# Where a projection stage issues its stores, and into which tiles it writes the lower halves of k

## The chip, the cores and the metric

The kernel runs on one core of one Trainium2 chip. The metric is the device time of one execution in microseconds. Engines are named as in the profile: PE (TensorE matmul), DVE (VectorE), ACT (ScalarE), POOL (GpSimd) and SP (SyncE, which here only issues DMAs); each works through its own instructions in order.

## The reference

One step of a one-layer streaming encoder over 1024 prompt tokens and 64 sample tokens, all in float32. What matters here is its first part, the combined input projection, and what is done at once with q and k:

```python
xn = _rmsnorm(x, p['norm_mix_w'])
proj = xn @ p['w_in']
z, xbc, dt_raw, q, k, v, gate_ssm, gate_att = jnp.split(proj, np.cumsum(IN_SIZES)[:-1].tolist(), axis=-1)
...
y_ssm = y_ssm * jax.nn.silu(z)
...
q = _partial_rope(_rmsnorm(q.reshape(b, t, 2 * ATT_HEADS, ATT_HEAD_DIM), p['q_norm_w']), q_pos)
k = _partial_rope(_rmsnorm(k.reshape(b, t, 2 * ATT_HEADS, ATT_HEAD_DIM), p['k_norm_w']), q_pos)
```

k after norm and rotation is also an output. q and k, and the cached keys, are used later by the attention, which this kernel multiplies in split precision: a float32 array is held as an upper half (cast to TensorE's rounded type) and a lower half (the rest).

## The kernel before

**The stage of pairs.** q, k and z are projected in 16 pairs of 256 output columns (`in_pair`, L636), q first, then k, then z. A pair is a two-by-two blocked product made of seven block products instead of eight, each in two column ranges s, so it has 14 steps; a step is 12 matmuls (`pile`, L642: four blocks of the inner dimension by three terms upper-upper, upper-lower, lower-upper) into one PSUM bank. Step by step the results are combined: p0 is copied by ACT into u1 (L685), p1 is added by DVE into u2 (L687), p3 into u1 (L689), and p2, p4, p5, p6 give the four finished blocks of a pair (ACT L695, DVE L697) in tiles `pre`. p2 and p3 go on accumulating into the banks of p0 and p1, so PE can start them only after L685 and L687 have read what stands there.

**The weights** of the next pair are loaded by SP (L552), combined by POOL (`ws` and `w_f`, L563 to L569), and split by ACT (cast to `wh` or `w_hi`, L419) and DVE (the rest, to `wh` or `w_lo`, L420).

**Finished rows.** `done` (L660) applies Silu to a finished block of z (L666), or adds the squares of q's and k's rows up (L673 to L677), and stores the block to a DRAM scratch: `z_sc`, `q_r` or `k_r` (L678, 64 stores of 272 KB, issued by SP).

**Norm, rotation and split of q, k and the cached keys** ride beside the pairs that follow. `finishing` (L802) and `cached_keys` (L876) make one generator `job` (L760) per piece: 24 pieces of 128 rows (`part`, twelve of q and twelve of k), 8 of two row blocks that are rotated (`turned`, four each), and 8 of cached keys. A job fetches its rows into a tile x on POOL's queue (L830; L846 and, for the rotation's cosines, L847; L880), waits four turns, scales x on DVE (L834, or L854 and the rotation L858 to L861, with a helper tile rt), stores it, for k alone, as the output `kT` (L769, on SP), waits a turn, casts the upper half on ACT (L773) into a tile xh (or rt), stores it (L774, SP, 40 stores), waits two turns (four for k), subtracts in place on DVE to leave the lower half in x (L777), and stores that (L778, SP). For k, L777 therefore waits until the store of x to the output has read x. A turn is one step of a pair; `take_turn` (L782) advances every running job at each step.

**Tiles.** `row(tag, name)` (L476) hands out 1088 columns of a ring of buffers: "fx" has four (x, and n1), "fc" three (xh, sq, rt, rp and others), "fp" three (`pre`). A tile's first writer waits for the last reader of the tile that had the buffer before. The order on each engine is as the steps record it, except that `after(...)` (L161) pins a block's instructions behind the named ones recorded last.

**Semaphores of DMAs.** The DMAs of SP and ACT take turns in eight semaphores, so an issue also waits for the one some eight issues before it to have landed.

Of the kernel before, what the change touches and what calls it, by code (L numbers as in the profile page):

```python
# [9 lines left out]
F32 = mybir.dt.float32  # L10
R32 = mybir.dt.float32r
# [6 lines left out]
P = 128  # L18
# [72 lines left out]
def hybrid_layer(ctx: ExitStack, tc: tile.TileContext, xT, xt, prm, cst, rope, wvd, win, wbs, wba, wout, wup, wdn,  # L91
# [2 lines left out]
    V, S, G, PE = nc.vector, nc.scalar, nc.gpsimd, nc.tensor  # L94
    act = S.activation
    load = nc.sync.dma_start

    dram = ctx.enter_context(tc.tile_pool(name="dram", bufs=1, space=DRAM))
    cp = ctx.enter_context(tc.tile_pool(name="cp", bufs=1))
# [376 lines left out]
    def row(tag, name, dt=F32):  # L476
        if tag in ("fa", "fs", "fu"):
            w = {"fa": KT * P, "fs": 4 * P, "fu": HT}[tag]
            return rows_l.tile([P, w], dt, name=name, tag=tag, bufs=IN_ROWS[tag])
        w = {"ss": T}.get(tag, HT)  # L480
        return rows_r.tile([P, w], dt, name=name, tag=tag, bufs=IN_ROWS[tag])
# [154 lines left out]
    def in_pair(n):  # L636

        kind, j = INPUT[n]
        u1, u2 = row("fx" if n == 1 else "fu", "u1"), row("fu", "u2")
        banks, out = {}, {}  # L640

        def pile(key, p, s, start):  # L642
            if start:
                banks[key, s] = acc(W2[s])
            ps, w, b = banks[key, s], left[n][p], parts[PARTS[p], s]
            for k in range(4):
                c = slice(P * k, P * (k + 1))
                for i, (x, y) in enumerate(((0, 0), (0, 1), (1, 0))):
                    seen["mm"] = PE.matmul(ps, w[x][:, c], b[y][:, k], start=start and k == i == 0, stop=k == 3 and i == 2,
                                           skip_group_check=not start)  # L650
            return ps

        def to(r, c, s):

            if (r, c) not in out:
                out[r, c] = row("fp", "pre")
            a, w = O2[s], W2[s]
            return out[r, c][:, a : a + w]

        def done(r, c):  # L660
            cs = slice(HT * c, HT * (c + 1))
            t = out[r, c][:, :HT]
            f = 2 * j + r
            if kind == "z":
                with after("root"):
                    seen["silu"] = act(t, t, AF.Silu)  # L666
            else:
                if kind not in squares:
                    squares[kind] = row("ss", "ss")
                ss = squares[kind][:, cs]  # L670
                if (kind, c) not in begun_squares:
                    begun_squares.add((kind, c))
                    act(ss, t, AF.Square)  # L673
                else:
                    sq = row("fc", "sq")[:, :HT]
                    act(sq, t, AF.Square)
                    V.tensor_tensor(out=ss, in0=ss, in1=sq, op=ALU.add)  # L677
            load(out={"z": z_sc, "q": q_r, "k": k_r}[kind][P * f : P * (f + 1), cs], in_=t)  # L678

        at = yield  # L680
        for _ in range(14):
            p, s = at
            us = cols(s)
            if p == 0:
                seen["copy"] = S.copy(u1[:, us], pile("a", p, s, True))  # L685
            elif p == 1:
                seen["read"] = V.tensor_tensor(out=u2[:, us], in0=pile("b", p, s, True), in1=u1[:, us], op=ALU.add)  # L687
            elif p == 3:
                seen["read"] = V.tensor_tensor(out=u1[:, us], in0=pile("b", p, s, False), in1=u1[:, us], op=ALU.add)  # L689
            else:  # L690
                r, c, key, start, u = {2: (0, 0, "a", False, None), 4: (1, 1, "c", True, u1), 5: (1, 0, "d", True, u1),
                                       6: (0, 1, "c", False, u2)}[p]
                ps = pile(key, p, s, start)
                if u is None:
                    seen["copy"] = S.copy(to(r, c, s), ps)  # L695
                else:
                    seen["read"] = V.tensor_tensor(out=to(r, c, s), in0=ps, in1=u[:, us], op=ALU.add)  # L697
                if s == 1:
                    ripe.append(lambda r=r, c=c: done(r, c))
            at = yield  # L700
# [56 lines left out]
                    return  # L757
            yield 2

    def job(fetch, scale, hi_of, hi_rows, lo_rows, keep=None):  # L760

        x = fetch()
        yield 4
        hi = lambda: None
        if scale is not None:
            with after("read"):
                x = scale(x)
            if keep is not None:
                load(out=keep, in_=x)  # L769
            yield 1  # L770
        with after("copy"):
            hi = hi_of()
            S.copy(hi, x)  # L773
        load(out=hi_rows, in_=hi.bitcast(F32))  # L774
        yield 2 if keep is None else 4
        with after("read"):
            V.tensor_tensor(out=x.bitcast(R32), in0=x, in1=hi, op=ALU.subtract)  # L777
        load(out=lo_rows, in_=x)  # L778

    running, clock = [], [0, 0, 0]  # L780

# [20 lines left out]
    def finishing(kind):  # L802

        d, to, keep, wcol = {"q": (q_r, q_st, None, lambda j: wq8[:, j : j + 1]),
                             "k": (k_r, k_st, kT, lambda j: col(O_KN + j))}[kind]
        rs = squares[kind]
        for (c, w), gap in zip(WIDE, (2, 2, 1)):
            ps = stat(w)
            with tc.issue_after(seen["mm"].ins):
                PE.matmul(ps, blk, rs[:, c : c + w], start=True, stop=True)  # L810
            with after("copy"):
                S.copy(rs[:, c : c + w], ps)
            yield gap
        while kind == "k" and clock[2] not in (6, 7, 8):
            yield 1
        with after("copy", *(["silu"] if "silu" in seen else [])):
            table = S.preload_act_table_set(LN_EXP)
        with tc.issue_after(table.ins):
            for c, w in WIDE:
                t = [row("fx", "n1") for _ in range(2)]  # L820
                rstd_of(None, rs[:, c : c + w], rs[:, c : c + w], w, "qn", 1.0 / 64, t=t)
        yield 3

        def rows_at(y, r0, j, n, c, w):
            return y[r0 + P * j : r0 + P * (j + n), c : c + w].rearrange("(j p) t -> p j t", p=P)

        def part(j, c):
            def fetch():
                x = row("fx", "x")
                G.dma_start(out=x, in_=d[P * j : P * (j + 1), c : c + HT])  # L830
                return x

            def scale(x):
                V.scalar_tensor_tensor(x, x, wcol(j), rs[:, c : c + HT], ALU.mult, ALU.mult)  # L834
                return x.unsqueeze(1)

            at = j, 1, c, HT
            return job(fetch, scale, lambda: row("fc", "xh", R32)[:, :HT].unsqueeze(1), rows_at(to, 0, *at), rows_at(to, D, *at),
                       None if keep is None else rows_at(keep, 0, *at))

        def turned(c):
            t = None

            def fetch():
                x, cosine = couple(row("fx", "x")), couple(row("fc", "rp"))
                G.dma_start(out=x, in_=d[0 : 2 * P, c : c + QW].rearrange("(j p) t -> p j t", p=P))  # L846
                G.dma_start(out=cosine, in_=rope[:, :, c : c + QW])  # L847
                return x, cosine

            def scale(both):  # L850
                nonlocal t
                x, cosine = both
                for j in range(2):
                    V.scalar_tensor_tensor(x[:, j], x[:, j], wcol(j), rs[:, c : c + QW], ALU.mult, ALU.mult)  # L854
                co, si = (cosine[:, i].unsqueeze(1).to_broadcast([P, 2, QW]) for i in range(2))
                t = row("fc", "rt")
                y = couple(t)
                V.tensor_tensor(out=y, in0=x, in1=si, op=ALU.mult)  # L858
                V.tensor_tensor(out=x, in0=x, in1=co, op=ALU.mult)
                V.tensor_tensor(out=x[:, 0], in0=x[:, 0], in1=y[:, 1], op=ALU.subtract)  # L860
                V.tensor_tensor(out=x[:, 1], in0=x[:, 1], in1=y[:, 0], op=ALU.add)  # L861
                return x

            at = 0, 2, c, QW
            return job(fetch, scale, lambda: couple(t.bitcast(R32)), rows_at(to, 0, *at), rows_at(to, D, *at),
                       None if keep is None else rows_at(keep, 0, *at))

        for j in range(2, KT):
            yield part(j, 0)
            yield part(j, HT)  # L870
            yield 1
        for c in range(0, T, QW):
            yield turned(c)
            yield 2
# [1095 lines left out]
```

## Time and profile before

| | us |
|---|---|
| median of 3 runs | 2435.89 |
| lowest and highest of them | 2434.46, 2437.45 |
| the profiled execution's own time | 2433.65 |
| its span | 2431.9 |
| PE busy in the span | 2390.7 |
| DVE, ACT, POOL busy | 1716.9, 1213.1, 692.3 |
| mean granted clock of TensorE | 0.996 of full speed |

The stage of pairs lies between about 115 and 481 us of the span. The profile counts an instruction of an engine as busy; idle time just before it is shown in square brackets in the timeline, with what ended it. DMA-issuing instructions stand on the issuing engine's queue (`SPq`, `POOLq`), with the time that the issue took there; "us to landing" is from the issue to the arrival of the data. Line numbers are those of the kernel before.

### The profile page before, as it was taken

How to read it: one execution, taken by the hardware profiler on the slowest of the kernel's cores; microseconds unless marked ns; L12 is line 12 of the kernel's file. 1: busy time of each engine (PE TensorE's matmuls, PEld its weight loads, DVE VectorE, ACT ScalarE, POOL GpSimd, SP SyncE). 2: the span in 40 equal slices, each digit the busy share in tenths (PEclk: the TensorE clock that was granted, in tenths of full speed). 3: DMA queues.
4: the chain of work that ended last, by engine and by line, in shares of the span. 5: the costliest groups of instructions: out<-in, count | busy, mean ns of one | idle time of the engine just before them, and what ended most of it. 6: DMA issues, size and time to landing. Idle time of an engine off the chain costs nothing. (4 is left out here: it accounts for less than half of the span.)

```text
span 2431.9 us, 49445 instructions
## 1 busy us (share of the span) xinstructions
PE 2390.7 (98%) x18744; PEld 2317.6 (95%) x18744; DVE 1716.9 (71%) x3090; ACT 1213.1 (50%) x2683; POOL 692.3 (28%) x757
## 2 busy tenths in 40 slices
PE   8999999999999999999999999999999999999998
PEld 8999999999999999998899998999999999999998
DVE  4678887668687786867678665756866756777765
ACT  7344454356565665657655553434444333353442
POOL 0032433201011010115343332013254554443344
PEclk9999999999999999999999999999999999999999
DMA  7863768665444444336797954664124424357975
GB/s 244 278 236 129 268 204 302 197 194 155 155 150 152 127 149 142 108 127 227 261 329 248 334 177 162 213 210 159 56 85 147 156 97 157 126 185 211 254 182 105
DMA packets 296240, 449.79 MB, mean 185 GB/s; under 512 B 36729, under 2 KB 192514, under 8 KB 296002
## 3 DMA queue, kind: packets, MB, share of 16 engines
q1 hardware_dynamic: 284962, 420.31, 52.3%
q0 software_dynamic: 11040, 26.34, 5.3%
q8 instruction: 147, 2.41, 0.4%
q14 instruction: 91, 0.75, 0.1%
HBM read 294.03 MB, written 152.50 MB: 184 GB/s over the span
## 5 line engine op out<-in xcount | busy, mean ns | idle before, releaser
L170 PE MATMUL mm<-b,w_hi 128*128 128x272 f32 x1576 | 465.8, 296 | 0.0
L172 PE MATMUL mm<-b,w_lo 128*128 128x272 f32 x1576 | 459.3, 292 | 0.0
L171 PE MATMUL mm<-b,w_hi 128*128 128x272 f32 x1576 | 458.0, 291 | 0.0
L170 PEld LDWEIGHTS mm<-b,w_hi 128*128 128x128 f32 x1576 | 296.9, 188 | 6.2 <-issue 5.1
L171 PEld LDWEIGHTS mm<-b,w_hi 128*128 128x128 f32 x1576 | 297.1, 189 | 2.9 <-issue 2.1
L172 PEld LDWEIGHTS mm<-b,w_lo 128*128 128x128 f32 x1576 | 296.5, 188 | 0.7 <-issue 0.2
L996 DVE SCALAR_TENSOR_TENSOR cc<-pre,par,cc 128x272 f32<-128x272 f32 (+1 forms) x288 | 140.0, 490 | 16.0 <-ACT cc L994 13.0
L1612 PE MATMUL mx<-n,wh 128*128 128x272 f32 x1080 | 144.9, 290 | 1.9 <-DVE u L1639 1.2
L1612 PE MATMUL mx<-m,w_hi 128*128 128x272 f32 x752 | 144.6, 289 | 0.2 <-DVE m L420 0.2
L984 POOL COPY pre<-pre 128x3 f32<-128x3 f32 x72 | 22.9, 318 | 418.5 <-DVE cc L998 198.4
L1612 PEld LDWEIGHTS mx<-n,wh 128*128 128x128 f32 x1080 | 139.7, 190 | 2.3 <-DVE u L1639 1.4
L170 PE MATMUL mx<-b,w_hi 128*128 128x272 f32 x472 | 138.8, 294 | 1.1 <-ACT w_hi L155 0.5
L172 PE MATMUL mx<-b,w_lo 128*128 128x272 f32 x472 | 137.7, 293 | 1.0 <-DVE w_lo L156 1.0
L1120 ACT ACTIVATE p_t<-sc,mx 128x512 f32<-128x512 f32 (+6 forms) x144 | 106.2, 740 | 64.4 <-DVE mx L1111 30.7
L156 DVE TENSOR_TENSOR w_lo<-w_f,w_hi 128x1024 fp32r<-128x1024 f32 (+1 forms) x82 | 102.2, 1247 | 50.6 <-ACT w_hi L155 49.6
L420 DVE TENSOR_TENSOR wh<-w_f,wh 128x512 fp32r<-128x512 f32 (+1 forms) x144 | 136.7, 950 | 0.7 <-ACT wh L419 0.7
L171 PE MATMUL mx<-b,w_hi 128*128 128x272 f32 x472 | 135.8, 288 | 0.0
L155 ACT CAST w_hi<-w_f 128x1024 fp32r<-128x1024 f32 (+1 forms) x82 | 85.9, 1048 | 70.0 <-PE mm L171 49.3
L1612 PEld LDWEIGHTS mx<-m,w_hi 128*128 128x128 f32 x752 | 118.1, 188 | 0.4 <-DVE m L420 0.4
L563 POOL TENSOR_TENSOR ws<-w_f 128x512 f32<-128x512 f32 (+1 forms) x47 | 63.1, 1342 | 176.4 <-DMA w_f<-in_wdn_dram 61.7
L1621 ACT ACTIVATE cc<-pre,par 128x544 f32<-128x544 f32 (+1 forms) x44 | 37.2, 846 | 147.9 <-DVE pre L1656 147.2
L1612 PE MATMUL mx<-m,w_lo 128*128 128x272 f32 x376 | 108.3, 289 | 0.0
(460 smaller groups left out, 7074.3 us busy)
## 6 DMA issues: line engine op xcount, KB each, us to landing
w_f<-in_win_dram SPq DMA_DIRECT2D x48, 512.0 KB, 4.3
w_f<-in_wup_dram SPq DMA_DIRECT2D x80, 256.0 KB, 2.6
bc<-a_sc SPq DMA_DIRECT2D x32, 512.0 KB, 5.6
w_f<-in_win_dram SPq DMA_DIRECT2D x60, 256.0 KB, 3.8
b<-y_sc SPq DMA_DIRECT2D x24, 544.0 KB, 8.3
h_sc<-hb SPq DMA_DIRECT2D x44, 272.0 KB, 2.1
ht<-h_sc SPq DMA_DIRECT2D x22, 544.0 KB, 4.5
t_sc<-ht SPq DMA_DIRECT2D x22, 544.0 KB, 2.9
```

The costliest lines, as they stand in the source:

```text
L155: S.copy(hi, w)
L156: V.tensor_tensor(out=lo, in0=w, in1=hi, op=ALU.subtract)
L170: PE.matmul(ps, a_hi, b_hi, start=i == 0, stop=False)
L171: PE.matmul(ps, a_hi, b_lo, start=False, stop=False)
L172: PE.matmul(ps, a_lo, b_hi, start=False, stop=i == n - 1)
L420: V.tensor_tensor(out=lo, in0=src, in1=hi, op=ALU.subtract)
L563: G.tensor_tensor(out=s1, in0=q21, in1=q22, op=ALU.add)
L984: G.tensor_copy(pre[:, 0:3], tail)
L996: V.scalar_tensor_tensor(cc[:, :m], pre[:, i : i + m], cw(i), cc[:, :m], ALU.mult, ALU.add)
L1120: act(p_t[:n, :nk], sc[c][:n, :nk], AF.Exp, bias=mx[:n, c : c + 1], accum_out=dst)
L1612: PE.matmul(ps, w[x][:, c], b[y][:, k], start=start and k == i == 0, stop=k == 3 and i == 2, skip_group_check=not start)
L1621: act(cc[:, :n], pre[h][:, :n], AF.Identity, bias=col(O_FB + f), scale=cw(0))
```

## The change

Four things, all in the stage of pairs:

- the 64 stores of finished rows (L678) are issued by ACT instead of SP;
- the 40 stores of upper halves (L774) are issued by ACT, pinned behind the cast as the cast is pinned;
- k's lower halves (L777) go into a tile of their own, `xl`: from the ring "fc" for the twelve pieces of 128 rows, from "fx" for the four rotated ones; the subtraction then stands two turns behind the cast for k as for the others, and no longer writes the tile that the store to `kT` reads;
- the stores left on SP stand a turn later: that of `kT` a turn behind the scale, that of the lower half a turn behind the subtraction.

```diff
+    send = nc.scalar.dma_start
...
-            load(out={"z": z_sc, "q": q_r, "k": k_r}[kind][P * f : P * (f + 1), cs], in_=t)
+            send(out={"z": z_sc, "q": q_r, "k": k_r}[kind][P * f : P * (f + 1), cs], in_=t)
...
-    def job(fetch, scale, hi_of, hi_rows, lo_rows, keep=None):
+    def job(fetch, scale, hi_of, hi_rows, lo_rows, keep=None, lo_of=None):
...
                 x = scale(x)
+            yield 1
             if keep is not None:
                 load(out=keep, in_=x)
-            yield 1
         with after("copy"):
             hi = hi_of()
             S.copy(hi, x)
-        load(out=hi_rows, in_=hi.bitcast(F32))
-        yield 2 if keep is None else 4
+            send(out=hi_rows, in_=hi.bitcast(F32))
+        yield 2
+        lo = x if lo_of is None else lo_of()
         with after("read"):
-            V.tensor_tensor(out=x.bitcast(R32), in0=x, in1=hi, op=ALU.subtract)
-        load(out=lo_rows, in_=x)
+            V.tensor_tensor(out=lo.bitcast(R32), in0=x, in1=hi, op=ALU.subtract)
+        yield 1
+        load(out=lo_rows, in_=lo)
...
-                       None if keep is None else rows_at(keep, 0, *at))
+                       *(() if keep is None else (rows_at(keep, 0, *at), lambda: row("fc", "xl")[:, :HT].unsqueeze(1))))
...
-                       None if keep is None else rows_at(keep, 0, *at))
+                       *(() if keep is None else (rows_at(keep, 0, *at), lambda: couple(row("fx", "xl")))))
```

The changed kernel's lines stand one to three further on (L777 is L779 there, L774 is L775, L858 is L861). PE's order is the same but for two places where a handful of its instructions stand a few places off. SP's program goes from 1286 rows to 1180, ACT's from 1978 to 2091.

DVE before, at the end of a pair beside which k is split: the last products' sums into `pre` (L697), then the splits of the next weights, then the sums L687 that PE waits for.

```order
L777 TENSOR_TENSOR x<-x,xh 128x544
L697 TENSOR_TENSOR pre<-mx,u_4378 128x272
L420 TENSOR_TENSOR wh<-w_f,wh 128x512
L834 SCALAR_TENSOR_TENSOR x<-x,par,ss 128x544
L777 TENSOR_TENSOR x<-x,xh 128x544
L420 TENSOR_TENSOR w_lo<-ws_4523,w_hi 128x512
L420 TENSOR_TENSOR w_lo<-w_f,w_hi 128x512
L687 TENSOR_TENSOR u_4648<-mm,u_4647 128x272
```

The same place after.

```order
L698 TENSOR_TENSOR pre<-mx,u_4378 128x272
L421 TENSOR_TENSOR wh<-w_f,wh 128x512
L779 TENSOR_TENSOR xl<-x,xh 128x544
L837 SCALAR_TENSOR_TENSOR x<-x,par,ss 128x544
L421 TENSOR_TENSOR w_lo<-ws_4526,w_hi 128x512
L421 TENSOR_TENSOR w_lo<-w_f,w_hi 128x512
L688 TENSOR_TENSOR u_4653<-mm,u_4652 128x272
```

One of the two subtractions has moved behind L687, and the other stands ahead of the scale and writes `xl`. Next, ACT before, at the end of the pair in which the last pieces of 128 rows meet the first rotated ones of k.

```order
L419 CAST wh<-w_f 128x512 x2
L773 CAST xh<-x 128x544
L666 ACTIVATE pre<-pre 128x544
L773 CAST xh<-x 128x544
L666 ACTIVATE pre<-pre 128x544 x2
L685 COPY u_5191<-mm 128x272
L419 CAST w_hi<-ws_5067 128x512
```

The same place after.

```order
L420 CAST wh<-w_f 128x512 x2
L774 CAST xh<-x 128x544
L775 DMA k_st<-xh 128x544
L667 ACTIVATE pre<-pre 128x544
L679 DMA z_sc<-pre 128x544
L774 CAST xh<-x 128x544
L667 ACTIVATE pre<-pre 128x544
L775 DMA k_st<-xh 128x544
L679 DMA z_sc<-pre 128x544
L667 ACTIVATE pre<-pre 128x544
L679 DMA z_sc<-pre 128x544
L686 COPY u_5204<-mm 128x272
```

Five DMA issues now stand between the casts and the copy of p0. The second cast takes its buffer of "fc" from the first cast's tile (the two buffers between went to an `xl` and to the cosines rp), so it waits until the first store has landed. Last, DVE before, two pairs further on than the first place, where the second rotated piece of k is finished.

```order
L854 SCALAR_TENSOR_TENSOR x<-x,par,ss 128x272 x2
L858 TENSOR_TENSOR rt<-x,rp 128x544
L859 TENSOR_TENSOR x<-x,rp 128x544
L777 TENSOR_TENSOR x<-x,rt 128x544
L860 TENSOR_TENSOR x<-x,rt 128x272
L861 TENSOR_TENSOR x<-x,rt 128x272
L689 TENSOR_TENSOR u_5191<-mx,u_5191 128x272 x2
L697 TENSOR_TENSOR pre<-mx,u_5191 128x272
```

And after.

```order
L857 SCALAR_TENSOR_TENSOR x<-x,par,ss 128x272 x2
L779 TENSOR_TENSOR xl<-x,rt 128x544
L861 TENSOR_TENSOR rt<-x,rp 128x544
L862 TENSOR_TENSOR x<-x,rp 128x544
L690 TENSOR_TENSOR u_5204<-mx,u_5204 128x272
L863 TENSOR_TENSOR x<-x,rt 128x272
L864 TENSOR_TENSOR x<-x,rt 128x272
L690 TENSOR_TENSOR u_5204<-mx,u_5204 128x272
L698 TENSOR_TENSOR pre<-mx,u_5204 128x272
```

The subtraction stands ahead of the next piece's rotation, and the first sum of p3 stands ahead of the rotation's last two instructions.

## The prediction

> **What bounds the kernel.** The page first: the span, and the busy time of the engines.
>
> ```profile
> span 2431.9 us, 49445 instructions
> PE 2390.7 (98%) x18744; PEld 2317.6 (95%) x18744; DVE 1716.9 (71%) x3090; ACT 1213.1 (50%) x2683; POOL 692.3 (28%) x757
> ```
>
> PE works 98% of the time, and the change takes no matmul away. It can only win time in which PE stands still in the stage of pairs, or add to it. So the second view is what PE waits for there, 110 to 490 us (columns: total us, times, longest).
>
> ```profile
> PE mx L649 <- DVE u L687: 3.9, 2, 2.4
> PE mx L649 <- DVE pre L697: 2.7, 2, 2.4
> PE mm L649 <- DVE u L687: 1.4, 1, 1.4
> ```
>
> All the other waits of that list are 1.0 us or less each. The third view, PE's timeline, gives these three rows four places of size (start, duration; in brackets the idle time just before).
>
> ```profile
> 309.37 0.89 PE L649 MATMUL mx<-t,wh 128*128 128x272 f32 x5 [2.35 <-DVE u L687]
> 377.66 0.52 PE L649 MATMUL mm<-t,wh 128*128 128x272 f32 x2 [1.35 <-DVE u L687]
> 421.82 0.89 PE L649 MATMUL mx<-t,wh 128*128 128x272 f32 x5 [1.56 <-DVE u L687]
> 433.54 0.60 PE L649 MATMUL mx<-b,w_hi 128*128 128x272 f32 x2 [2.40 <-DVE pre L697]
> ```
>
> The last one costs more than its idle time. The windows behind it (length, PE busy with its matmuls, granted clock, DMA share, GB/s), and one behind the gap of 309:
>
> ```profile
> 433.50:437.00 3.50, 3.46 (x16) 0.55 1.01 314
> 437.00:441.00 4.00, 4.00 (x33) 0.97 0.77 262
> 309.40:313.00 3.60, 3.60 (x29) 1.00 0.82 250
> ```
>
> Behind 2.40 us of idle the granted clock was 0.55 for 3.5 us, and 16 matmuls took 3.46/16 = 0.216 us each where they take 4.00/33 = 0.121 next: 16 x 0.095 = 1.5 us. Behind 2.35 us it stayed at 1.00. So the four places are worth 2.35 + 1.35 + 1.56 + 2.40 + 1.5 = 9.2 us, 0.38% of the time, and that is the ceiling of this change. A measurement of this kernel can tell about 0.2%, 4.9 us, from no change.
>
> The Trainium skill ("TensorE: Matmul & The Clock Gate", "What's actually happening") has the clock halved after an idle window of about 3.4 us. Here 2.40 us were enough, with less idle than the rule names; by the rule no gap of this size would cost clock, the ceiling would be 7.7 us, and no term of 1.5 us would stand below.
>
> **The change part by part.**
>
> *k's lower half in its own tile.* DVE's waits from 340 to 455 us, and DVE's timeline ahead of the gap at 377:
>
> ```profile
> DVE x L777 <- DMA out_dram<-x: 18.2, 8, 4.5
> ...
> 369.86 0.77 DVE L834 SCALAR_TENSOR_TENSOR x<-x,par,ss 128x544 f32<-128x544 f32 x1
> 374.43 1.62 DVE L777 TENSOR_TENSOR x<-x,xh 128x544 fp32r<-128x544 f32 x1 [3.80 <-DMA out_dram<-x]
> 377.18 0.43 DVE L687 TENSOR_TENSOR u<-mm,u 128x272 f32<-128x272 f32 x1
> ```
>
> L777 overwrites x, so it waits until the store of x has landed, and L687 stands behind it. Eight such waits come to 18.2 us of DVE, but DVE is 71% busy, and PE only stood still behind three of them. In the new order one subtraction stands behind L687 and the other is no longer bound to that store. Its new bound is its buffer of "fc", that is the store of an upper half some jobs earlier. If that comes late it delays L687 as before, but 3.80 us of wait stand against a gap of 1.35, so 2.4 us of it may remain. I take the whole gap: **-1.35** (bounds -1.35 and 0).
>
> *The gap at 433.* DVE's timeline ahead of it:
>
> ```profile
> 424.16 0.91 DVE L854 SCALAR_TENSOR_TENSOR x<-x,par,ss 128x272 f32<-128x272 f32 x2 [0.75 <-DMA x<-k_r]
> 426.24 0.72 DVE L858 TENSOR_TENSOR rt<-x,rp 128x544 f32<-128x544 f32 x1 [1.17 <-DMA rp<-in_rope_dram]
> 428.44 1.14 DVE L777 TENSOR_TENSOR x<-x,rt 128x544 fp32r<-128x544 f32 x1 [0.71 <-DMA out_dram<-x]
> 430.94 1.50 DVE L861 TENSOR_TENSOR x<-x,rt 128x272 f32<-128x272 f32 x1
> 433.07 0.42 DVE L697 TENSOR_TENSOR pre<-mx,u 128x272 f32<-128x272 f32 x1
> ```
>
> From L854 to L697 the chain holds 0.75 + 1.17 + 0.71 = 2.63 us of waits, each for a transfer, against a gap of 2.40. The 0.71 goes with the tile. x and the cosines are fetched by POOL once buffers of "fx" and "fc" are free; x's buffer no longer waits for the lower half's store, so 0.75 should go; the cosines' 1.17 may stay. But in the new order L689 also passes L860 and L861, one of them 1.50 us long. 0.71 + 0.75 + 1.50 = 2.96 is over 2.40, so the gap goes, and its half clock: -2.40 - 1.5 = **-3.9** (bounds -3.9 and 0).
>
> *ACT as issuer.* No DMA is issued from ACT in this trace, so the price must come from SP's rows of the same stores (ns: least, median, most), beside the time that ACT now waits, 110 to 490 us:
>
> ```profile
> L774 SPq DMA_DIRECT2D q_st<-xh x12: 319/323/1745, 248.8 to 299.6; - x12
> L774 SPq DMA_DIRECT2D k_st<-xh x12: 319/587/1034, 351.5 to 413.8; - x12
> L678 SPq DMA_DIRECT2D z_sc<-pre x32: 319/333/842, 311.5 to 482.2; - x32
> ...
> ACT wh L419 <- POOL ws L567: 48.2, 14, 6.5
> ACT w_hi L419 <- POOL w_f L565: 15.2, 6, 3.5
> ```
>
> 104 issues at 0.32 to 0.59 us are 33 to 61 us; over 16 pairs 6.5 issues and 2.1 to 3.8 us a pair. ACT waits 48.2/14 = 3.4 us for POOL's `ws` nearly once a pair, and six times 2.5 us for `w_f`. These waits cover the issues, so I take **0** for them; without that cover they would be 2.1 us a pair. Below zero they do not go by themselves: SP is freed of its waits, but what it loads sooner, the weights, are waited for by POOL and ACT, not by PE.
>
> *The gap at 422.* Here the change adds a wait. ACT's two casts, DVE's rows up to L687, and from 280 to 455 us the landing of an upper half's store (median from the issue):
>
> ```profile
> 409.81 0.64 ACT L773 CAST xh<-x 128x544 fp32r<-128x544 f32 x1
> 410.92 0.63 ACT L773 CAST xh<-x 128x544 fp32r<-128x544 f32 x1
> ...
> 417.32 1.61 DVE L777 TENSOR_TENSOR x<-x,xh 128x544 fp32r<-128x544 f32 x1 [3.18 <-DMA out_dram<-x]
> 418.86 0.71 DVE L858 TENSOR_TENSOR rt<-x,rp 128x544 f32<-128x544 f32 x1
> 421.34 0.43 DVE L687 TENSOR_TENSOR u<-mx,u 128x272 f32<-128x272 f32 x1
> ...
> k_st<-xh SPq DMA_DIRECT2D x12, 272.0 KB, 4.1
> ```
>
> Now the second cast waits for the landing of the first store, and L858 takes its rt buffer from the second cast's tile and waits for the landing of that one's store. The first cast ends at 410.45; + 4.1 = 414.55; the second cast 0.64, and Silu's slot behind it about 0.6: issue at 415.8, landing 419.9. From L858's start to L687's end it is 421.34 + 0.43 - 418.86 = 2.91 us, so L687 ends at 422.8 instead of 421.77: the wait for `kT` (3.18) is gone, and two landings in a row take its place. **+1.0**, a gap of 2.6. Behind ACT's waiting cast stand z's Silu and stores, and behind these the copy L685 and the `w_hi` casts of the next pair; DVE's L420 and L687 wait for those. Bounds: -1.56, if weights and pieces run ahead by the DVE time saved, and +3.0, with both landings a us longer.
>
> *The gap at 309.* The same, beside q, whose tiles haven't changed:
>
> ```profile
> 299.63 0.74 SPq L774 DMA_DIRECT2D q_st<-xh  x1
> 306.69 1.67 DVE L858 TENSOR_TENSOR rt<-x,rp 128x544 f32<-128x544 f32 x1 [1.49 <-DMA q_st<-xh]
> ...
> q_st<-xh SPq DMA_DIRECT2D x2, 272.0 KB, 5.6
> ```
>
> L858 waited for that store to land, 7.0 us after its issue. ACT issues it behind a Square and a store of k_r, about 301.3. With the 5.6 us that the two stores of 296 to 310 us took in the median it lands at 306.9: **+0.3**. Bounds: -2.35 if it lands in 5 us or less, +1.7 with the 7.0 us again.
>
> The Trainium skill ("DMA: Bandwidth & Descriptors", "Issuing engines are not separate DMA queues") says that issuing from several engines only saves the sequencer's time, since all run on the same DMA engines. By that a store issued 1.7 us later lands 1.7 us later, and this term would be the +1.7 and the sum below -1.05. No run here shows an issue from ACT yet.
>
> *Half clock.* Of two gaps of 2.35 and 2.40 one was followed by it. With two expected at about 2.6 I count it once: **+1.5**.
>
> **Sum**: -1.35 - 3.9 + 0 + 1.0 + 0.3 + 1.5 = -2.45 us. Against the profiled execution's own 2433.65 (2.2 below the median, its span 1.75 below itself) that is 2431.2; on the scale of the median, 2435.89 - 2.45 = **2433.4**.
>
> **The rivals.**
>
> *All gaps behind the removed wait go.* If the chain at 410 runs ahead of time, the gap at 422 goes too: -1.35 - 1.56 - 3.9 = -6.8, 2429.1; with the one at 309, 2426.7. For it: 18.2 us of DVE's waits go, and SP's queue loses these (110 to 490 us), so that weights and lower halves behind them are issued sooner.
>
> ```profile
> SPq L774 <- ACT xh L773: 37.3, 14, 6.0
> SPq L678 <- ACT pre L666: 30.7, 17, 7.6
> SPq L678 <- DVE pre L697: 28.3, 21, 3.3
> ```
>
>  Against it: the two landings in a row at 410 are there whatever else runs ahead.
>
> *Nothing moves.* The lower halves wait for their buffer in a ring of three which xh, rt, rp and now xl share, and DVE stands as long as before, for `k_st<-xh` instead of `out_dram<-x`: 0, 2435.9. For it, the store of an upper half lands in 4.1 us, not much sooner than that of x in the same list:
>
> ```profile
> out_dram<-x SPq DMA_DIRECT2D x16, 272.0 KB, 5.1
> ```
>
> Against it, one subtraction has left its place ahead of L687.
>
> *ACT becomes what is late.* An issue waits in ACT's order for its semaphore's earlier DMA; a wait of one landing (4.1) a pair on top of 2.1 us of issues, less the cover of 3.4, leaves ACT 2.8 us late, and with it the copies L685 and the `w_hi` casts, on which L420, L687 and PE stand. It decides as soon as ACT's delay in a pair exceeds 3.4 us. Beside k DVE has gained 18.2/8 = 2.3 a pair to set against it, beside q nothing: two pairs there at 2.8 with a half clock each are +8.6, with the sum above +6.2: 2442.
>
> **How the numbers follow.** The forecast, small gains against two later gaps: 0.30. All gaps go: 0.27. Nothing moves: 0.15. ACT late: 0.28. Faster by over 0.2% (under 2431.0) is the second alone, 0.27; within 0.2% the first and third, 0.45; slower (above 2440.8) 0.28. The range goes from the full gain, 2427.0, to 2443.0, a little over the third rival's price; a twentieth is left below and a seventh above, for more pairs than two. The forecast's own bounds are 2429 to 2437.
>
> **What would show it.** Right: no `out_dram<-x` among DVE's releasers for L777; no gap near 377 and 433; the ones near 309 and 422 still there, behind L687, with `q_st<-xh` and `k_st<-xh` as releasers of L858 and of the cast L773. Wrong on the fast side: those two gone. Wrong on the slow side: PE waiting for ACT's u L685 or for L420 once a pair, ACT idle before its issues, and windows with a granted clock of about half. The matmuls of the rest of the program should take what they took.

## The result, and the profile after

| | before | after |
|---|---|---|
| median of 22 runs, us | 2434.40 | 2429.14 |
| lowest and highest, us | 2427.17, 2438.01 | 2423.21, 2433.48 |
| ratio of the two, 95% interval | | 0.9982 (0.9975 to 0.9989) |
| profiled execution's own time, span, us | 2433.65, 2431.9 | 2427.86, 2426.1 |
| first matmul of the stage of pairs to the end of its last, us | 115.74 to 480.69: 364.95 | 117.93 to 473.33: 355.39 |
| TensorE's idle places in the stage from 200 us on, sum, us | 8.95 | 1.41 |

The kernel is faster by 0.18%, 2.7 to 6.1 us: a gain clear of scatter and a little under the 0.2% that the prediction drew as its line. (One execution of the variant e5 below took 5964 us; its ratio leaves it out.) The last two rows are from the trace: the first start and last end of the 2688 matmuls of `pile`, and the idle times of 0.12 us or more between TensorE's matmuls in the stage, from 200 us on.

What PE waits for in 200 to 480 us after the change (total us, times, longest), the whole list:

```profile
PE mx L650 <- DVE pre L698: 0.8, 1, 0.8
PE st L729 <- DVE st L724: 0.6, 1, 0.6
PE sc L1109 <- DMA q<-q_st: 0.4, 1, 0.4
```

The two rows for L687 (L688 in the new numbering) are gone, and of L697's 2.7 us one wait of 0.8 is left. Three of the four gaps are gone, the two that should have stayed or grown among them. What is left of the one near 433 is this, 4.6 us earlier in the span (PE's row, and the DVE row ahead of the sum L698 that PE waits for):

```profile
428.95 0.51 PE L650 MATMUL mx<-b,w_hi 128*128 128x272 f32 x2 [0.76 <-DVE pre L698]
...
424.92 3.63 DVE L779 TENSOR_TENSOR xl<-x,rt 128x544 fp32r<-128x544 f32 x1
```

This one subtraction took 3.63 us, where most others of its kind took 0.72; POOL combined weights for 2.56 us of that time. Whether the one slows the other no run here tested.

DVE's waits from 340 to 455 us, the first lines:

```profile
DVE xl L779 <- ACT xh L774: 5.2, 3, 2.4
DVE xl L779 <- DMA k_st<-xh: 3.9, 2, 2.8
```

`out_dram<-x` (18.2 us before) has left the list. The subtraction now waits for its own cast, and twice for a buffer of "fc", for the store of an upper half.

What an issue costs on ACT's queue (ns: least, median, most) could not be read before:

```profile
L775 ACTq DMA_DIRECT2D q_st<-xh x12: 326/326/914, 251.0 to 300.3; - x12
L775 ACTq DMA_DIRECT2D k_st<-xh x12: 326/326/332, 351.4 to 409.9; - x12
...
L679 ACTq DMA_DIRECT2D z_sc<-pre x32: 326/326/1319, 312.0 to 474.9; - x32
```

and ACT's timeline shows what it takes from ACT's own work:

```profile
289.09 0.65 ACT L774 CAST xh<-x 128x544 fp32r<-128x544 f32 x1 [2.32 <-DVE x L837]
289.65 0.38 ACT L696 COPY pre<-mx 128x272 f32<-128x272 f32 x1
289.77 0.33 ACTq L775 DMA_DIRECT2D q_st<-xh  x1
289.92 0.62 ACT L420 CAST wh<-w_f 128x512 fp32r<-128x512 f32 x1
...
405.46 0.33 ACTq L775 DMA_DIRECT2D k_st<-xh  x1
405.83 0.66 ACT L667 ACTIVATE pre<-pre 128x544 f32<-128x544 f32 x1 [0.40 <-ACT xh L774]
```

At 289.77 the cast whose data are stored had just ended (289.09 + 0.65 = 289.74), with a copy already started between the two; the issue lies beside that copy, and the next cast follows as if there were none. At 405.46 the issue stands directly behind its cast, and ACT's next instruction came 0.40 us after the cast's end. So in these rows an issue whose data are ready costs ACT 0 to 0.40 us, not a fixed 0.33. (An issue that must wait can cost more, as e9 shows below.)

Where the rest of the time went. The stage is 9.6 us shorter between these two profiles, the span only 5.8. The stage started 2.2 us later (117.93 against 115.74) and what follows it took 1.4 us more (1943.2 against 1941.7, the end of its last matmul to the end of the program's). The start looks like scatter: over the 14 profiles of this study the stage starts at 114.9 to 117.9 us, without regard to which queue issues what. For what follows the stage, see the end of the experiments.

### The profile page after: what moved, and what is told of

Its sections match the earlier page's. It is cut to its first block, busy times and chain, and to the rows that moved or that the text cites. A ratio compares the mean times of both kernels' runs of the same rounds, so it can differ in the third digit from the quotient of the medians.

```text
span 2426.1 us, 49374 instructions
## 1 busy us (share of the span) xinstructions
PE 2388.9 (98%) x18744; PEld 2316.9 (96%) x18744; DVE 1725.6 (71%) x3090; ACT 1214.9 (50%) x2683; POOL 694.2 (29%) x757
## 4 chain that ended last, share of the span: by engine, by line
PE 48%; DVE 3%; DMA 1%; issue 1%; ACT 1%; POOL 0%; SPq 0%; POOLq 0%; DVEq 0%; ACTq 0%
PE mx L1615 13%; PE mx L1789 6%; PE mm L1615 5%; PE mx L171 3%; PE mx L173 3%; PE mx L172 3%; PE mm L171 3%; PE mm L173 3%; PE mm L172 3%; PE mm L1789 2%; PE yi L1304 1%; PE ye L1310 1%; PE stp L1316 1%; DMA bc<-a_sc 1%; DVE m L421 1%
## 5 line engine op out<-in xcount | busy, mean ns | idle before, releaser
L999 DVE SCALAR_TENSOR_TENSOR cc<-pre,par,cc 128x272 f32<-128x272 f32 (+1 forms) x288 | 140.1, 490 | 15.4 <-ACT cc L997 12.5
```

What stands on the lines that cost most here:

```text
L999: V.scalar_tensor_tensor(cc[:, :m], pre[:, i : i + m], cw(i), cc[:, :m], ALU.mult, ALU.add)
```

## Experiments

All are compared with the kernel before on their own chip; each also left one profile. "Stage" is the row of the table above; "gaps" its last row, and "start" the start of the stage's first matmul. Theory A was that k's tile pays, B that SP's emptied queue pays. The stages of e1, e2, e3, e4, e7 and e10 hold a stretch of half clock near 134 us, and those of before, e6 and e8 one behind a gap, each worth about 1.5 us by the prediction's estimate; the other five hold none.

| kernel | rows by | halves by | own tile | later stores | ratio (95%) | stage | start | gaps |
|---|---|---|---|---|---|---|---|---|
| before | SP | SP | no | no | 1 | 365.0 | 115.7 | 9.0 |
| e8 | ACT | SP | no | no | 0.9998 (0.9988 to 1.0009) | 364.9 | 115.4 | 8.7 |
| e7 | SP | ACT | no | no | 0.9993 (0.9984 to 1.0002) | 366.4 | 116.2 | 9.5 |
| e1 | ACT | ACT | no | no | 0.9984 (0.9976 to 0.9993) | 356.9 | 117.0 | 3.5 |
| e9 (kT by ACT) | SP | SP | no | no | 0.9989 (0.9979 to 0.9999) | 358.7 | 116.7 | 4.3 |
| e2 | SP | SP | yes | no | 0.9989 (0.9979 to 0.9998) | 357.7 | 115.1 | 3.3 |
| e6 | SP | SP | yes | yes | 0.9987 (0.9977 to 0.9997) | 358.8 | 116.7 | 4.2 |
| e4 | ACT | SP | yes | yes | 0.9986 (0.9976 to 0.9995) | 356.3 | 117.0 | 2.7 |
| e5 | ACT | ACT | yes | no | 0.9976 (0.9966 to 0.9985) | 359.2 | 115.1 | 4.6 |
| e3, e10 | SP | ACT | yes | yes | 0.9969 (0.9958 to 0.9980), 0.9967 (0.9955 to 0.9980) | 353.0, 354.6 | 114.9, 117.5 | 0.4, 1.8 |
| after, e11 | ACT | ACT | yes | yes | 0.9982 (0.9975 to 0.9989), 0.9975 (0.9964 to 0.9986) | 355.4, 356.0 | 117.9, 115.2 | 1.4, 2.2 |
| e12 (all by ACT) | ACT | ACT | yes | yes | 0.9978 (0.9967 to 0.9988) | 354.2 | 115.4 | 1.0 |

**e1, the sends alone.**

```diff
-            load(out={"z": z_sc, "q": q_r, "k": k_r}[kind][P * f : P * (f + 1), cs], in_=t)
+            send(out={"z": z_sc, "q": q_r, "k": k_r}[kind][P * f : P * (f + 1), cs], in_=t)
...
             S.copy(hi, x)
-        load(out=hi_rows, in_=hi.bitcast(F32))
+            send(out=hi_rows, in_=hi.bitcast(F32))
```

> Only the 104 stores go to ACT's queue; k's lower half stays in x and the stores left on SP keep their places. Measure: TensorE's idle time in 100 to 500 us of the trace (12.8 us before, 5.3 us in the changed kernel) and the ratio to before (0.9982 for the changed kernel). Theory A, k's own tile is what pays: DVE still waits for the store of x, the gaps near 377, 422 and 433 stay at 1.3 us or more each; idle 10 to 13 us, ratio 0.999 to 1.001. Theory B, SP's emptied queue is what pays, since weights come sooner: at least two of these three gaps go, idle 5 to 8 us, ratio 0.997 to 0.9985. On a third question, whether a second issuing queue costs something at the start of the program: if it does, the first idle place of the stage (125.0 us before, 127.2 us in the changed kernel) lies at 126.5 us or later here.

Measured: 0.9984, idle 6.2 us, stage 356.9. These are B's numbers: nothing is left near 377, 422 and 433, one gap of 1.19 is new at 440 and the one near 318 has grown from 0.38 to 1.38. But DVE still waits for the store of x, though less (from 340 to 455 us):

```profile
DVE x L778 <- DMA out_dram<-x: 11.8, 6, 4.4
```

**e2, the tile alone**, two turns behind the cast, with `lo_of` handed over as in the change; all stores stay SP's.

```diff
-        yield 2 if keep is None else 4
+        yield 2
+        lo = x if lo_of is None else lo_of()
         with after("read"):
-            V.tensor_tensor(out=x.bitcast(R32), in0=x, in1=hi, op=ALU.subtract)
-        load(out=lo_rows, in_=x)
+            V.tensor_tensor(out=lo.bitcast(R32), in0=x, in1=hi, op=ALU.subtract)
+        load(out=lo_rows, in_=lo)
```

> Only k's lower halves get tiles of their own, two turns behind the cast; all stores on SP at their old places. Theory A: the gaps near 377 and 433 go, and with them the half clock; idle 6 to 9 us (the gap near 309 beside q stays, 2 us or more), ratio 0.997 to 0.9985. Theory B: the gap near 377 alone goes, idle 10 to 12 us, ratio 0.999 to 1.000. Start of the program: no second queue here, so the stage's first idle place at 125 us if the second queue is what moved it, anywhere from 124 to 128 us if it is scatter.

Measured: 0.9989, just outside A's ratio, idle 5.9 us, just under A's range, stage 357.7. Near 377 and 422 nothing is left, of the gap near 433 0.86, of the one near 309, beside q, 1.31, where A had 2 or more. Beside k that is A's picture. Both theories hold with the other's part left out, so the parts don't add: either takes most of the gaps beside k away.

**e3 and e4, the change with one kind of store back on SP.**

```diff
-            send(out={"z": z_sc, "q": q_r, "k": k_r}[kind][P * f : P * (f + 1), cs], in_=t)
+            load(out={"z": z_sc, "q": q_r, "k": k_r}[kind][P * f : P * (f + 1), cs], in_=t)
```

> The changed kernel with the 64 stores of finished rows back on SP; the 40 stores of upper halves stay on ACT. Theory A: as the changed kernel beside k, idle 5.3 to 6.5 us, ratio 0.9975 to 0.9990. Theory B: SP stands behind the finished rows again (59 us of such waits before), weights come late, one or two of the four gaps return at 1 us or more: idle 7 to 10 us.

Measured: 0.9969, idle 3.1 us, stage 353.0: better than either theory had it, though the interval of the ratio reaches into A's range.

```diff
             S.copy(hi, x)
-            send(out=hi_rows, in_=hi.bitcast(F32))
+        load(out=hi_rows, in_=hi.bitcast(F32))
```

> The changed kernel with the 40 stores of upper halves back on SP; the 64 stores of finished rows stay on ACT. Theory A: as the changed kernel beside k; the gap near 309 hangs on the landing of q's upper half, which SP issues as soon as the cast is done: 0 to 2.4 us. Idle 5.3 to 8 us. Theory B: SP waits for casts again (37 us before), so about half of the gain is lost, idle 8 to 10 us.

Measured: 0.9986, idle 4.8 us, under both ranges, stage 356.3: no gap above 0.72 us returns, against B.

**e5 and e6.** From here on there is a theory C: the gaps are the end of one chain that is some us late, and any relief of it takes them away; the rival D gives each part its own gap. e5 takes the later stores out of the change:

```diff
                 x = scale(x)
-            yield 1
             if keep is not None:
                 load(out=keep, in_=x)
+            yield 1
...
-        yield 1
         load(out=lo_rows, in_=lo)
```

> The changed kernel without its fourth part: the store of x to the output right behind the scale and that of the lower half right behind the subtraction, as before. Theory C, the gaps are one chain a few us too late and any relief of it takes them away, so that gains don't add: stage of pairs as in the changed kernel (355.4 us from its first matmul to its last; 365.0 before), 354 to 358 us, ratio 0.9975 to 0.9990. Rival D, each part of the change has a gap of its own: then the later stores should own one, and a gap of 1 us or more comes back. Rows of q, k and z are on ACT here: if that is what made the stage start late in the three runs that had it (117.0 to 117.9 us against 114.9 to 115.7 in the three that hadn't), it starts at 117 us or later; if that was scatter of the start of the program, anywhere from 114.8 to 118.

Measured: ratio 0.9976, as in C, but in its profile a gap of 2.34 at 427 and one of 1.39 at 316, stage 359.2, outside C's range, as in D. Its ratio is no worse than the changed kernel's, so one profile isn't enough to give the later stores a gap of their own. The stage started at 115.1: the start doesn't follow the queue.

e6 takes both kinds of stores back to SP, as the two diffs above, of e3 and e4, together.

> The changed kernel with all 104 stores back on SP: own tiles for k's lower halves, and the later stores. Theory C: as the tiles alone (357.7 us, of which 1.5 are a half clock at 130 us), stage 355 to 358 us, ratio 0.9980 to 0.9995. Rival D: the gap near 309 beside q remains whole, 2 us or more, and the sum of gaps from 200 to 480 us is that of the tiles alone, 3.6 us, or more. Start of the stage 114.8 to 116 us if rows on ACT are what moves it.

Measured: 0.9987, stage 358.8, a little above C's range, of which a half clock and 2.50 us near 309. Beside k it is C (0.19 and 0.87 us left near 422 and 433), beside q D.

**e7 and e8, half of the sends.** The kernel before with only the second, or only the first, of e1's two edits.

> The kernel before with one thing changed: the 40 stores of upper halves go to ACT's queue. Theory C: the pieces run a little ahead and the gaps go although DVE still waits for the store of x: stage 354 to 358 us, ratio 0.9975 to 0.9990. Rival D: gaps near 377, 422 and 433 stay (5.3 us), only the one near 309 may go: stage 361 to 365 us, ratio 0.999 to 1.000. Start of the stage 114.8 to 116 us if rows on ACT are what moves it.

> The kernel before with one thing changed: the 64 stores of finished rows go to ACT's queue. Theory C: SP is free of 59 us of waits, weights come sooner, the gaps go: stage 354 to 358 us, ratio 0.9980 to 0.9995. Rival D: the gaps beside k stay, stage 361 to 365 us. If rows on ACT cost something by themselves (the kernel that had halves and tiles but kept the rows on SP was the fastest, 0.9969, stage 353.0 us), the stage is no shorter than 358 us and it starts at 117 us or later.

Measured: 0.9993 and 0.9998, both not told apart from no change, stages 366.4 and 364.9, gaps of 2.42 and 2.24 us near 422. C fails here. D had these two about right but not their sum: the two halves, neither of which gives anything that can be told from scatter, give 8 us of the stage together in e1. What C lacked is seen on SP's queue ahead of the gap at 422 in the kernel before: DVE's scale and its later subtraction, and SP's issues between them.

```profile
408.72 1.11 DVE L834 SCALAR_TENSOR_TENSOR x<-x,par,ss 128x544 f32<-128x544 f32 x1
417.32 1.61 DVE L777 TENSOR_TENSOR x<-x,xh 128x544 fp32r<-128x544 f32 x1 [3.18 <-DMA out_dram<-x]
```

```profile
410.48 0.32 SPq L774 DMA_DIRECT2D k_st<-xh  x1
410.90 0.37 SPq L552 DMA_DIRECT2D w_f<-in_win_dram  x1
411.36 0.42 SPq L778 DMA_DIRECT2D k_st<-x  x1
411.88 0.45 SPq L678 DMA_DIRECT2D z_sc<-pre  x1
412.42 1.25 SPq L769 DMA_DIRECT2D out_dram<-x  x1
```

x was scaled at 409.83. SP stood at a store of an upper half until ACT's cast was done (409.81 to 410.45), and three more issues had piled up behind that one: 0.65 us of waiting and 1.94 us of issues, so the store of x was issued 2.6 us late. The same job in e1, where SP has neither kind (DVE, then SP):

```profile
405.71 0.77 DVE L835 SCALAR_TENSOR_TENSOR x<-x,par,ss 128x544 f32<-128x544 f32 x1
408.31 0.71 DVE L778 TENSOR_TENSOR x<-x,xh 128x544 fp32r<-128x544 f32 x1
...
412.39 0.71 DVE L778 TENSOR_TENSOR x<-x,xh 128x544 fp32r<-128x544 f32 x1
```

```profile
406.51 0.34 SPq L770 DMA_DIRECT2D out_dram<-x  x1
```

Issued 0.03 us after the scale, and the subtraction at 412.39 waits for nothing. Over the 16 stores to kT the mean lateness is 0.78 us before, with 2.5 to 3.1 us for four of them; 0.54 with the rows alone moved and 0.55 with the halves alone, the worst 2.6 and 2.1; 0.05 with both, the worst 0.35. At the store ahead of the gap at 422 it is 2.6, 2.1, 2.1 and 0.03. There each kind of store was enough to hold SP up, so both had to leave.

Only one of the four late stores stands directly ahead of a gap. The subtractions ahead of the other two gaps waited for stores that were 1.1 us late (the one ahead of 377, issued at 367.58 and landed at 374.34) and not late at all (the one ahead of 433, issued at 422.49, 0.03 us behind its rotation):

```profile
367.58 0.65 SPq L769 DMA_DIRECT2D out_dram<-x  x1
```

So the expectation of e9 goes too far where it says that 2.5 to 3.1 us were lost at each place where a gap follows.

**e9, the store of x alone.** This tests it without the other 104 stores:

```diff
-                load(out=keep, in_=x)
+                send(out=keep, in_=x)
```

> The kernel before with one thing changed: the 16 stores of x to the output kT go to ACT's queue; everything else, the subtraction in place with its wait for that store too, stays. Before, SP issued these stores 0.78 us after the scale in the mean, and 2.5 to 3.1 us after it at the places where a gap follows, since it stood waiting at a store of an upper half or of a finished row; with both kinds on ACT it was 0.05 us, with one of them 0.55. Theory F, this lateness is what makes the gaps beside k: issued at 0 to 0.3 us after the scale, DVE's wait for these stores falls from 18.2 to 12 us or less, the gaps near 377, 422 and 433 come to 2 us or less together (5.3 before), stage of pairs 357 to 361 us (365.0 before), ratio 0.9980 to 0.9995. Rival G, what paid was that weights come sooner from a free SP: gaps as before, stage 363 to 367 us, ratio 0.9995 to 1.001.

Measured: 0.9989, stage 358.7, DVE's wait 9.5 us:

```profile
DVE x L778 <- DMA out_dram<-x: 9.5, 8, 3.8
```

Near 377, 422 and 433 0.71, 0 and 0.62 us are left, 1.3 of 5.3. Those are F's numbers for the gaps, the wait and the time, with sixteen DMAs moved instead of 104. One number of F is missed, and it is the one that was to be the cause: the lateness is 0.96 us in the mean. ACT holds five stores up by 1.4 to 4.7 us, but others than SP did: at the four stores that were 2.5, 2.5, 3.1 and 2.6 us late before it is 3.0, 0, 1.4 and 0, and with them the time from the scale to the landing went from 7.8, 7.0, 9.0 and 7.4 us to 7.8, 4.9, 5.8 and 5.8. So G's numbers did not come, and the lateness is shown as a cause for the gap at 422 alone, where DVE's wait fell from 3.18 to 1.62 us; that the other two shrink is shown, by which step is not.

What is left at 377 has a cause of its own, and it is the third rival of the prediction. The issue on ACT at 372.67 waited until an earlier DMA of its semaphore, a store of a lower half by SP, had landed (372.60), and ACT's copy, DVE and PE stood behind it:

```profile
372.67 0.34 ACTq L770 DMA_DIRECT2D out_dram<-x  x1
373.05 0.39 ACT L686 COPY u<-mm 128x272 f32<-128x272 f32 x1 [3.18 <-DMA k_st<-x]
...
373.99 1.58 DVE L421 TENSOR_TENSOR w_lo<-w_f,w_hi 128x512 fp32r<-128x512 f32 x1 [3.12 <-ACT w_hi L420]
...
375.97 1.27 PE L650 MATMUL mm<-t,wh 128*128 128x272 f32 x8 [0.71 <-DVE u L688]
```

A gap of 1.16 at 441 is new.

**e10 and e11, once more.** e3's kernel and the changed kernel, on one chip.

> The changed kernel with the finished rows' stores on SP once more, beside the changed kernel on one chip. If it is really faster than the changed kernel: 0.9965 to 0.9975, stage 352 to 355 us. If its first run was scatter: 0.9975 to 0.9990, stage 354 to 359 us.

> The changed kernel once more, for a second profile and as the neighbour of the run before: ratio 0.9975 to 0.9990, stage 354 to 359 us; its first gap list (nothing above 1 us from 200 to 480 us) should be the same if the gaps are gone for good, one of 1 to 2.5 us should show near 309, 422 or 433 if they only sit at the edge.

Measured: 0.9967 and 0.9975, medians 2424.57 and 2427.00 us of six runs each, stages 354.6 and 356.0. The variant with the finished rows left on SP beats the kernel before clearly, by 0.31 to 0.33%, and was ahead of the changed kernel both times, but the intervals overlap: that it beats the changed kernel is likely, not shown. What an extra 64 issues on ACT would cost isn't seen in the profiles either. In e11's list nothing in the stage is above 0.64 us: in both profiles of the changed kernel the gaps are gone.

**e12, everything on ACT.** The change with the last two `load` of `job` made `send` as well.

> The changed kernel with the stage's other 56 stores, those of lower halves and of kT, on ACT too: 160 issues instead of 104. Theory C with ACT's idle time as cover (48 us of waiting for POOL's ws before): nothing moves, stage 354 to 359 us, ratio 0.9975 to 0.9995. Rival, ACT in order is close to being what is late: the stores of kT and of the lower halves make ACT wait for DVE, the copy L686 and the casts of weights come late, PE waits for ACT u L686 or DVE u L688 by 3 us or more from 200 to 480 us, stage 360 us or more, ratio 0.9995 or above.

Measured: 0.9978, stage 354.2, gaps 1.0. ACT is no bound with 160 issues either: from 200 to 480 us PE waits for DVE and for one load, 0.5 us or less each time, and for ACT not at all. From 110 to 490 us ACT still waits for POOL:

```profile
ACT wh L420 <- POOL ws L568: 33.4, 11, 3.9
```

**What stays open.** By the profiles the stage lost 9 to 12 us in the best kernels, by the runs the program lost 4 to 8. A profile is one execution, and not always a typical one: e3's was the fastest of its seven runs, 3.9 us under their median, and e12's the fastest of twelve, 5.2 us under. The part behind the stage took 1940.2 to 1942.4 us in the three profiles whose stage is long (before, e7, e8) and 1941.0 to 1945.3, in the mean 1943.0, in the eleven whose stage is short. Of these 1.6 us some 1.1 can be half clock: behind the stage the three have 2.0 stretches of it in the mean and the eleven 2.7, at an estimated 1.5 us each, from the stretch at 433. If the 1.6 us are real, something later gives back a part of the gain; the difference lies within the scatter of single profiles, and no run here tells the two apart.

## Why the prediction was right, and where it was not

The forecast was 2433.4 on a median of 2435.89, -2.45 us; measured were -2.7 to -6.1. The sign was right, and the measured ratio, -4.4, lies between the forecast and the first rival's -6.8. The path was right in part only. By the prediction's own signs the fast side came true: the gaps near 309 and 422 are gone, and the stage lost the whole price of that rival with both gaps (9.2). Two terms, +1.0 and +0.3, had the wrong sign. That the time still came near the forecast is in part luck: the program gained only about half of what the stage did in the profiles, and why is open.

**The ceiling** (9.2 us) was near but was not one: the stage got 9.6 us shorter in one profile of the changed kernel, 8.9 in the other (e11) and 12.0 in e3. The four places are not all of PE's idle time; in the whole stage the places of 0.12 us or more come to 12.2 us before, without the half clock.

**The gap at 377**, -1.35: right, by the mechanism named. DVE no longer waits for the store of x; two waits for `k_st<-xh` came in its place (3.9 us), and none reaches PE. With the tile alone (e2) this gap is gone too.

**The gap at 433**, -3.9: right in sign, 0.76 us left of 2.40 and no half clock. The first sum of p3 now runs ahead of the rotation's last instructions, as the order showed, and the three waits of 2.63 us are gone. But in e1, where tile and order are as before, the gap is gone as well, with two of those waits still there (1.01 and 0.79 us): a head start is enough for it, and for the changed kernel the runs don't separate that from the terms of this sum.

**ACT as issuer**, 0: right, for a second reason that no row could show before. The cover was there (ACT still waits 38.8 us for POOL's `ws`), and an issue whose data are ready can also lie beside ACT's running instruction. The third rival, ACT late, did not come in the changed kernel, nor in e12. Its mechanism shows once: in e9 it cost PE 0.71 us. (In e8 PE stood 2.22 us for ACT's copy, but there ACT's Square had waited 2.68 us for a store that SP had issued.)

**The gap at 422**, +1.0: here the prediction failed. The two landings in a row are there. ACT's timeline after:

```profile
404.79 0.64 ACT L774 CAST xh<-x 128x544 fp32r<-128x544 f32 x1
405.46 0.33 ACTq L775 DMA_DIRECT2D k_st<-xh  x1
...
409.24 0.65 ACT L774 CAST xh<-x 128x544 fp32r<-128x544 f32 x1 [2.74 <-DMA k_st<-xh]
409.79 0.66 ACT L667 ACTIVATE pre<-pre 128x544 f32<-128x544 f32 x1
409.92 0.33 ACTq L775 DMA_DIRECT2D k_st<-xh  x1
```

and DVE's behind it, where L861 starts 0.18 us after the second store landed (414.20):

```profile
414.38 0.73 DVE L861 TENSOR_TENSOR rt<-x,rp 128x544 f32<-128x544 f32 x1 [2.08 <-issue]
415.02 0.69 DVE L421 TENSOR_TENSOR w_lo<-ws,w_hi 128x512 fp32r<-128x512 f32 x1
415.62 0.72 DVE L862 TENSOR_TENSOR x<-x,rp 128x544 f32<-128x544 f32 x1
416.26 0.69 DVE L421 TENSOR_TENSOR w_lo<-w_f,w_hi 128x512 fp32r<-128x512 f32 x1
416.86 0.43 DVE L688 TENSOR_TENSOR u<-mx,u 128x272 f32<-128x272 f32 x1
```

From the first cast to L688's end it is 417.29 - 404.79 = 12.5 us, where 13.0 had been forecast (422.8 - 409.81) and 11.96 were taken before. The chain's length was right. Its start was not: the prediction put the first cast where it had stood, at 409.81. Of the 5.0 us between 409.81 and 404.79 2.8 are PE's own advance by then: the same matmul starts 2.8 us sooner in the span, since the gaps ahead of it are gone. Counted from PE's place, the first cast starts 2.2 us sooner. L688 ends at 417.29, and PE would have stood from 417.43 on, so the margin is small (in e11 a gap of 0.56 is left here, in e4 one of 0.60). So the gap goes, by the bound -1.56 ("if weights and pieces run ahead") that was named and not taken; that was the first rival's condition, given 0.27. Waits that PE doesn't see, 18 us of DVE's and nearly 100 of SP's, were counted as worth nothing where PE did not stand behind them, but with them gone the pieces ran ahead, and that is the head start of this chain.

**The gap at 309**, +0.3: wrong too. Issue on ACT, then the wait for it on DVE:

```profile
300.32 0.48 ACTq L775 DMA_DIRECT2D q_st<-xh  x1
```

```profile
306.32 1.14 DVE L861 TENSOR_TENSOR rt<-x,rp 128x544 f32<-128x544 f32 x1 [0.59 <-DMA q_st<-xh]
307.99 0.43 DVE L688 TENSOR_TENSOR u<-mx,u 128x272 f32<-128x272 f32 x1
```

The store was issued at 300.32 instead of the forecast's 301.3, while the Square that stands ahead of it on ACT was still running, and it had landed 6.0 us later. PE, 2.0 us later there than before (the later start, less the gap at 203 that went), needed L688 at 307.02 + 2.0 = 309.0 and found it done at 308.4. The forecast had kept PE's place and DVE's fixed. This gap sits at the edge: with the same instructions beside q it was 2.35 before and 1.31 in e2. With both kinds of stores on SP and the later ones (e6) it was 2.50, with the halves alone on ACT (e7) 2.09; with the rows alone (e8) one of 2.22 stood 4 us ahead of it, behind ACT's copy; in all the others it is 0.5 us or less. What q's stores gained from the change is not settled by these runs beyond that.

**The rule on issuing engines** (the Trainium skill, "DMA: Bandwidth & Descriptors", "Issuing engines are not separate DMA queues") would have made the gap at 309 worse by its lateness. Landings did not get shorter, which agrees with the rule: the upper halves of k took 4.1 us from SP in the median of 280 to 455 us, and after

```profile
k_st<-xh ACTq DMA_DIRECT2D x12, 272.0 KB, 5.3
```

So what the moved stores gain is time on the issuing engine. But that time was not small here: not the 0.3 us of one issue, but the 2.6 us that a store stood behind one that wasn't ready and the issues piled up behind that.

**Half clock**, +1.5: none in the stage in either profile of the changed kernel, since no gap of its size was left; see below.

## What to carry to other kernels

A queue in order is as late as the least ready transfer in it: before counting what an issue costs, look at what stands ahead of it and how long that waits. Where two kinds of transfers held a third one up, moving either of them gave nothing that could be told from scatter; moving the third one, sixteen DMAs here, gave 6.3 us of the stage, and moving both 8.0. And a wait that no bound engine sees still sets where the next chain starts: when such waits go, work the later chains out from their new start, not from the old one.

## What the runs showed of the hardware that was not expected

The half clock doesn't follow the length of a gap. In nine of the 14 profiles the granted clock fell to half in the stage, for 3.41 us and at an estimated price of 1.5 us: in six of them behind the same two gaps of 0.99 and 0.61 us near 132, which all 14 have, of this same length; behind a single gap of 2.40 (before), 2.22 (e8) and 2.50 (e6); and not behind 2.35 (before), 2.34 (e5), 2.42 (e7) and 2.24 (e8).

What fits all of these is where a gap falls. Up to the program's last matmuls, the stretches of half clock of one profile start whole multiples of 3.413 us apart (before: 433.83, 1164.28, 1727.48 and 2205.35, that is 214, 379 and 519 times 3.413 behind the first), and each is one such slot long, or two. Cut the stage into these slots, and look at how many matmuls PE runs in the slot ahead (columns as in the prediction; a full slot has some 28). Before, the gap of 2.40 lies whole in one slot, and that of 2.35 lies in two, as e5's of 2.34 does (the last two rows):

```profile
430.42:433.83 3.41, 1.01 (x8) 1.00 0.37 100
433.83:437.24 3.41, 3.41 (x17) 0.50 0.97 334
307.54:310.95 3.41, 1.58 (x12) 1.00 0.60 202
310.95:314.37 3.42, 3.42 (x29) 1.00 0.87 271
425.83:429.24 3.41, 1.71 (x14) 1.00 0.66 213
429.24:432.66 3.42, 2.78 (x22) 1.00 0.91 230
```

Over the stages of the 14 profiles eight slots have ten matmuls or fewer that start in them, and half clock followed each; of two with eleven it followed one, and of those with twelve or more none. Behind the stage, where matmuls have other shapes, some slots with eight were not followed by it. This is read from traces; no run was made to test it. The Trainium skill ("TensorE: Matmul & The Clock Gate", "What's actually happening") speaks of a free-running window of about 3.4 us; that it runs free agrees with this, that it must be idle as a whole does not.
